# Forming a layer's sample states four heads at a time inside a feed-forward block, instead of beside a run of projections

## The chip, the core and the metric

The kernel runs on one core of one Trainium2 chip. The metric is device microseconds of one execution. The kernel before was timed at 1905.67 us, the median of three runs (1899.02, 1905.67 and 1908.37 us). The engines are named as in the profile: PE is the matrix engine (PEld its weight loads), DVE the vector engine, ACT the scalar engine, POOL the GpSimd engine and SP the engine whose queue issues nearly all transfers. Each engine works through its own instructions strictly in the order in which they were written to it. A semaphore holds an instruction back until what it needs is done, and holds back all that stands behind it on that engine too.

## The reference, cut to what matters

Two layers are computed for 512 prompt tokens and 8 sample tokens with shared weights. Layer 0 mixes with attention and a state-space model, layer 1 with a gated delta rule (16 value heads, 128 by 128 state each). A SwiGLU block (1024 to 2816 and back) follows each layer. For a sample token, the delta rule is one step per head:

```python
def step(s, inp):
    u0_c, kcd_c, attn_c, qg_c, kdec_c, gl_c = inp
    u = u0_c - jnp.einsum('bhik,bhkv->bhiv', kcd_c, s)
    o = jnp.einsum('bhik,bhkv->bhiv', qg_c, s) + jnp.einsum('bhij,bhjv->bhiv', attn_c, u)
    s = s * gl_c[..., None, None] + jnp.einsum('bhjk,bhjv->bhkv', kdec_c, u)
    return s, o
```

With one token per sample, the new state of a head is the old state times a decay, plus the outer product of the key and the vector u. The new states of 8 samples and 16 heads (128 by 128 each, 8.4 MB in all) are an output of the program, `sgs`. Nothing else in the program reads them: the sample's output `o` is worked out earlier from the old states.

## The kernel before

Activations lie transposed: 128 partitions by 520 columns (512 prompt, 8 sample), worked on in two halves of 256 and 264 columns. Every weight matrix is multiplied in three passes of float32r. A weight tile of 4 by 128 rows and 128 columns is split into a high part `whi` (a cast, L317 on ACT or L318 on DVE) and the remainder `wlo` (a subtraction, L193 on POOL or DVE), and each pair of tiles meets the two parts of the activations in three matmuls. One output tile of 128 features with eight k-tiles is 48 matmuls (8 k-tiles, 3 passes, 2 halves), all at L296 (`lin`). Raw weights come by 1 MB loads into two buffers, `raw`. There are four buffers of `whi` and of `wlo`, so the splits run at most four ahead of PE.

Layer 1 ends with its z projections: 16 tiles, each read out of PSUM and gated by `l1_gate` (the intermediate tiles `sq`, with the last product written as `p` or `X`). Beside the first of them `l1_sample` runs the samples' step against the old states, and leaves the vectors u in DRAM (`ud`). In the kernel before, `l1_sample_state` stands in program order between the two groups of eight z tiles. It takes 16 steps, one per sample and half of the heads. A step loads 8 heads of old state into `Hh` (512 KB), loads u spread to all partitions into `cs` (512 KB), multiplies by the decay on POOL (128 by 1024 elements), adds key times u in four DVE instructions (128 by 256 each, L309), and stores 512 KB.

Then come the output projection (768 matmuls with `w_gdn_out`), the norms, and the second feed-forward block, `ffn(1)`. It opens with a group: two gate tiles and two up tiles, run half after half so that PE has work while the norm of the second half is unfinished. The group's second up-weights borrow `b4` and `cs` as split buffers. Ten rounds follow, p from 1 to 10, each of two gate tiles and two up tiles; then comes the down projection. In this block every cast of a weight tile is on DVE, and so are two of three remainders; POOL has the third. DVE also reads the results out of PSUM.

The order of the instructions on each engine is set at build time. A scheduler walks the program with its own estimate of durations and appends to each engine whichever instruction it thinks is ready first. Where it thinks that a result will be there, it may place the instruction that needs it ahead of others.

Of the kernel before, what the change touches and what calls it, by code (L numbers as in the profile page):

```python
# [13 lines left out]
ALU = mybir.AluOpType  # L14
# [6 lines left out]
NS = 8  # L21
# [103 lines left out]
def KN(n, v, *others):  # L125

    return KNOBS.get(n, v)
# [95 lines left out]
class Ker:  # L223
# [103 lines left out]
    def lin(s, w, xh, xl, nkt, halves=(0, 1), ps=None):  # L327

        ps = ps or {h: s.acc()[:, 0:HW[h]] for h in halves}
        for n, (kt, hi, lo) in enumerate(w):  # L330
            for lhs, x, st, sp in ((hi, xh, n == 0, False), (hi, xl, False, False), (lo, xh, False, n == nkt - 1)):
                for h in halves:
                    s.mm(ps[h], lhs, x(kt, h), st, sp)
        return ps
# [752 lines left out]
    def ffn(s, l):  # L1087
        nc = s.nc
        g, u, d = s.i["w_ffn_gate"][l], s.i["w_ffn_up"][l], s.i["w_ffn_down"][l]
# [24 lines left out]
        s.lo_pool = KN("lp_f%d" % l, 1, 2, 3)  # L1114
        s.hi_v = KN("hv_f%d" % l, 0, 2, 3, 4, 1)
        if l:
            s.new_small()
            sgs = s.small(NT)
        for p in range(11):
            sg = {}  # L1120
            for t in (2 * p, 2 * p + 1):
                ps = first[t] if p == 0 else s.lin(s.W.tile(g, 128 * t, kts), *x, 8, ps=spare(t < 2 + KN("ma_f%d" % l, 0, 1, 2)))
                for h in (0, 1):
                    sl = (s.B("cs", NT * (t % 2), NT) if l == 0 else sgs if t % 2 else s.accT)[:, HALF[h]]
                    gt = s.tmp(HW[h])
                    with s.tc.high_priority():
                        s.tt(gt, ps[h], s.R2[:, HALF[h]], ALU.mult)
                    with s.tc.issue_after(s.norm_ins):
                        ins = s.act(sl, gt, AF.Silu)
                    sg[t, h] = sl  # L1130
                if l == 0 and p:
                    s.W.park(ins)
            for t in (2 * p, 2 * p + 1):
                ps = first[2 + t] if 2 + t < len(first) else s.lin(s.W.tile(u, 128 * t, kts), *x, 8)
                for h in (0, 1):
                    gt = s.tmp(HW[h])
                    with s.tc.high_priority():
                        s.tt(gt, sg[t, h], ps[h], ALU.mult)
                    a = hh(t, h)
                    ins = s.act(a, gt)  # L1140
                    s.tt(hl(t, h), gt, a.bitcast(F32), ALU.subtract)
                if l == 0 and p:
                    s.W.park(ins)
        while l == 0 and s.W.wait != [None, None]:
            s.W.park(ins)
        s.gen("Hh")
# [97 lines left out]
    def l1(s):  # L1244
        nc = s.nc
# [94 lines left out]
        for g in range(2):  # L1340
            hi, lo = (("p0", "X"), ("p2", "p7"))[g]
            s.gen(hi, lo)
            for j in range(8):
                s.l1_gate(g, j, lin(4096 + 128 * (8 * g + j)), s.lay(hi), s.lay(lo))
            if g == 0:
                s.l1_sample_state()
        s.l1_sample_gate()
        s.X = s.B("p5", 0, KD, NT)
        s.reload()
# [508 lines left out]
            nc.scalar.copy(hi, m)  # L1858
            s.tt(lo, m, hi.bitcast(F32), ALU.subtract)

    def l1_sample_state(s):
        nc, i, o = s.nc, s.i, s.o
        dap = lambda d: d if isinstance(d, bass.AP) else d[:]
        ud = dap(s.ud)
        gb = s.B("ex", 0, 8, 2, 16)
        s.dma(gb, dap(s.sgd).rearrange("(o b) w h -> o b w h", o=1).to_broadcast([128, 8, 2, 16]))
        for n in range(2 * NS):
            b, e = n // 2, n % 2
            S, ub = s.B("Hh", 1024 * (n % 4), 8, 128), s.B("cs", 1024 * (n % 2), 8, 128)
            s.dma(S, i["state_gdn"][0, b, 8 * e:8 * e + 8].rearrange("h k v -> k h v"))  # L1870
            s.dma(ub, ud[b:b + 1, 8 * e:8 * e + 8].to_broadcast([128, 8, 128]))
            s.tt(S, S, gb[:, b, 0, 8 * e:8 * e + 8].unsqueeze(2).to_broadcast([128, 8, 128]), ALU.mult, s.eng(KN("ss%d" % (n % 4), "G", "V")))
            for j in range(4):
                s.stt(S[:, 2 * j:2 * j + 2], ub[:, 2 * j:2 * j + 2], s.kqs[:, 4 * e + j, b, 0:1], S[:, 2 * j:2 * j + 2], ALU.mult, ALU.add)
            s.dma(o["sgs"][0, b, 8 * e:8 * e + 8].rearrange("h k v -> k h v"), S)

def build(tc, ins, outs, stop=None):
# [45 lines left out]
```

## Time and profile before

| what | value |
|---|---|
| median of three runs | 1905.67 us |
| the profiled execution | 1902.11 us, span 1900.3 us |
| mean granted PE clock | 0.961 of full |
| PE busy | 1747.3 us (92%) |
| DVE, ACT, POOL busy | 1180.4 us (62%), 769.5 us (40%), 891.5 us (47%) |
| bytes moved | 300.38 MB, mean 158 GB/s |
| z projections end, output projection runs | about 1374 us to 1478 us of the span |
| gate and up tiles of the second feed-forward | about 1488 to 1722 us |

A row of the table by stages gives the length of a stretch, then the busy time of each engine with the number of its instructions in brackets, then the granted PE clock, the busy share of the 16 DMA engines and the rate of transfers. A row of the timeline gives the start, the length, the engine, the line, the operation with output and inputs, and in square brackets the idle time just before it and what ended that. A row of the chain of waits gives start, length and what the end of the program hung on then. The busy time of PE is modelled and says little; how many matmuls fall in a stretch says more.

### The profile page before, as it was taken

Reading aid. Unit: us, or ns where it says so; the run is one execution under the profiler, and the core shown is the slowest. Engines: PE = TensorE matmul, PEld = TensorE weight load, DVE = VectorE, ACT = ScalarE, POOL = GpSimd, SP = SyncE. Lnnn points to the kernel's source line nnn. Section 1 sums busy time; section 2 is a strip of 40 time slices with the busy share of each in tenths; the row PEclk is TensorE's granted clock in tenths of the full one; section 3 lists DMA queues with packets and bytes.
Section 4 is the critical chain, followed back from the end, with each engine's and each line's share of the span. In section 5 each row is a group of like instructions: output and inputs, shape, how many; then the busy total and the mean of one; then the engine's idle time right before and its main releaser. Section 6 shows DMA issues by size and latency. Waiting matters only on the chain.

```text
span 1900.3 us, 36580 instructions
## 1 busy us (share of the span) xinstructions
PE 1747.3 (92%) x14263; PEld 1660.3 (87%) x14263; DVE 1180.4 (62%) x2325; ACT 769.5 (40%) x1868; POOL 891.5 (47%) x777
## 2 busy tenths in 40 slices
PE   7889999798999999989977798988899899999996
PEld 6888777598999999979977797977789899999996
DVE  6898878538433321178799958888954955453125
ACT  4442245555333333346766565554334411111222
POOL 2465757234666653342343564545668411112452
PEclk8999999898999999999988999999989899999998
DMA  7335765453565553356752123266998333333544
GB/s 259 124 120 179 227 204 165 135 171 108 167 189 182 180 170 93 92 153 211 245 173 84 46 68 93 56 180 188 279 288 229 134 133 134 134 134 128 158 158 151
DMA packets 325967, 300.38 MB, mean 158 GB/s; under 512 B 13761, under 2 KB 299142, under 8 KB 324626
## 3 DMA queue, kind: packets, MB, share of 16 engines
q1 hardware_dynamic: 325142, 297.37, 50.7%
q8 instruction: 112, 1.84, 0.4%
q10 hardware_dynamic: 652, 0.68, 0.1%
q14 instruction: 61, 0.50, 0.1%
HBM read 261.98 MB, written 72.52 MB: 176 GB/s over the span
## 4 chain that ended last, share of the span: by engine, by line
PE 52%; DVE 19%; DMA 7%; ACT 4%; issue 3%; POOL 1%; SPq 0%; DVEq 0%; ACTq 0%; POOLq 0%
PE acc L296 46%; PE ma L296 3%; DVE p L302 3%; PE mb L296 2%; DVE sq L309 2%; DVE cs L309 2%; DMA raw<-in_w_ffn_down_dram 2%; DVE b L302 1%; ACT L312 1%; DVE wlo L193 1%; DVE Hh L309 1%; DVE Hl L309 1%; DVE p L309 1%; DVE p L1496 1%; PE mb L299 1%
## 5 line engine op out<-in xcount | busy, mean ns | idle before, releaser
L193 POOL TENSOR_TENSOR wlo<-raw,whi 128x512 fp32r<-128x512 f32 (+2 forms) x342 | 456.2, 1337 | 594.1 <-ACT whi L317 296.7
L296 PE MATMUL acc<-Hl,whi 128*128 128x256 f32 (+1 forms) x2576 | 564.5, 292 | 36.1 <-DVE cs L302 18.0
L296 PEld LDWEIGHTS acc<-Hl,whi 128*128 128x128 f32 x2576 | 420.7, 193 | 53.1 <-issue 20.5
L317 ACT CAST whi<-raw 128x512 fp32r<-128x512 f32 (+3 forms) x392 | 234.8, 603 | 436.4 <-PE acc L296 343.6
L296 PE MATMUL acc<-Hh,whi 128*128 128x256 f32 (+1 forms) x1824 | 387.0, 287 | 3.8 <-DVE cs L302 2.0
L296 PE MATMUL acc<-Hh,wlo 128*128 128x256 f32 (+1 forms) x1824 | 389.4, 288 | 0.0
L296 PEld LDWEIGHTS acc<-Hh,whi 128*128 128x128 f32 x1824 | 292.7, 191 | 8.3 <-issue 4.8
L296 PEld LDWEIGHTS acc<-Hh,wlo 128*128 128x128 f32 x1824 | 293.2, 191 | 7.6 <-issue 6.7
L296 PE MATMUL acc<-bm,whi 128*128 128x256 f32 (+1 forms) x1136 | 236.1, 291 | 0.1
L296 PE MATMUL acc<-p,whi 128*128 128x264 f32 (+1 forms) x1280 | 230.0, 287 | 3.9 <-ACT p L1858 1.6
L318 DVE CAST whi<-raw 128x512 fp32r<-128x512 f32 x131 | 61.7, 472 | 253.2 <-PE acc L296 195.9
L193 DVE TENSOR_TENSOR wlo<-raw,whi 128x512 fp32r<-128x512 f32 (+1 forms) x141 | 112.9, 802 | 140.6 <-ACT whi L317 135.5
L296 PEld LDWEIGHTS acc<-p,whi 128*128 128x128 f32 x1280 | 190.3, 192 | 5.6 <-ACT p L1858 1.9
L296 PEld LDWEIGHTS acc<-bm,whi 128*128 128x128 f32 x1136 | 182.9, 195 | 2.4 <-issue 1.6
L296 PE MATMUL acc<-Hl,wlo 128*128 128x256 f32 (+1 forms) x752 | 171.1, 297 | 1.0 <-DMA wlo<-pk 0.5
L296 PE MATMUL acc<-p,wlo 128*128 128x256 f32 (+1 forms) x704 | 164.0, 287 | 8.0 <-DVE wlo L193 7.1
L296 PEld LDWEIGHTS acc<-Hl,wlo 128*128 128x128 f32 x752 | 127.6, 198 | 3.3 <-issue 1.2
L296 PEld LDWEIGHTS acc<-p,wlo 128*128 128x128 f32 x704 | 119.5, 192 | 9.2 <-DVE wlo L193 7.9
L296 PE MATMUL acc<-X,whi 128*128 128x264 f32 (+1 forms) x512 | 100.1, 290 | 2.6 <-DVE X L302 1.3
L309 DVE SCALAR_TENSOR_TENSOR cs<-cs,cw 128x512 f32<-128x512 f32 x100 | 90.6, 906 | 12.0 <-POOL cs L302 7.0
L296 PEld LDWEIGHTS acc<-X,whi 128*128 128x128 f32 x512 | 80.3, 195 | 4.1 <-ACT X L312 2.4
L309 DVE SCALAR_TENSOR_TENSOR Hh<-cs,CS,Hh 128x256 f32<-128x256 f32 x64 | 53.2, 894 | 26.9 <-POOL Hh L302 26.7
(467 smaller groups left out, 3010.0 us busy)
## 6 DMA issues: line engine op xcount, KB each, us to landing
raw<-in_w_gdn_in_dram SPq DMA_DIRECT2D x24, 1024.0 KB
raw<-in_w_ffn_gate_dram SPq DMA_DIRECT2D x22, 1024.0 KB
raw<-in_w_ffn_up_dram SPq DMA_DIRECT2D x22, 1024.0 KB
raw<-in_w_ffn_down_dram SPq DMA_DIRECT2D x20, 1024.0 KB
raw<-in_w_hyb_in_dram SPq DMA_DIRECT2D x16, 1024.0 KB
out_sv_dram<-in_cache_attn_v_dram SPq DMA_DIRECT2D x16, 1023.0 KB
out_sk_dram<-in_cache_attn_k_dram SPq DMA_DIRECT2D x16, 1023.0 KB
cs<-in_w_gdn_in_dram SPq DMA_DIRECT2D x40, 256.0 KB
```

The source lines that it names most:

```text
L193: eng.tensor_tensor(out=lo[:, :nk, d:d + n], in0=raw[:, :, o:o + n], in1=hi[:, :nk, d:d + n].bitcast(F32), op=ALU.subtract)
L296: s.nc.tensor.matmul(out, lhsT=lhsT, rhs=rhs, start=start, stop=stop, skip_group_check=skip)
L299: s.nc.tensor.transpose(out, in_, s.ident[0:in_.shape[0], 0:in_.shape[0]])
L302: return (eng or s.nc.vector).tensor_tensor(out=out, in0=a, in1=b, op=op).ins
L309: return s.nc.vector.scalar_tensor_tensor(out=out, in0=a, scalar=sc, in1=b, op0=op0, op1=op1).ins
L312: return s.nc.scalar.activation(out=out, in_=in_, func=f, **kw).ins
L317: return s.nc.scalar.copy(out, in_).ins
L318: return (s.nc.vector if e == "V" else s.nc.gpsimd).tensor_copy(out, in_).ins
L1496: nc.vector.transpose(out=xt[pr], in_=A[pr, :, pr].rearrange("p y j -> p j y"))
```

## The change

The new states are no longer formed beside the z projections. `l1_sample_state` becomes a generator, `state_steps`, which the second feed-forward advances by one step after each tile of rounds 1 to 10, until its 34 turns are used up. The pieces are half as large: 32 steps of four heads. A turn stores the states of two steps ago, computes the step before, and loads the next one. A step has one state load, one load of u and one store (256 KB each), one POOL multiplication of 128 by 512, and two DVE instructions of 128 by 256. States lie in four buffers of `cs`, u in two buffers of `b4` that the opening group's weights used, and the decays in the small tile instead of `ex`. The multiplications are on POOL, as before. The bytes and the arithmetic are the same as before; only the number of instructions differs: 32 POOL instructions of half the size in place of 16, the same 64 on DVE, 96 transfers of 256 KB in place of 48 of 512 KB.

```diff
@@ ffn
         if l:
+            s.gen("cs")
             s.new_small()
             sgs = s.small(NT)
+            states = s.state_steps()
...
                 if l == 0 and p:
                     s.W.park(ins)
+                if l and p:
+                    next(states, None)
...
                 if l == 0 and p:
                     s.W.park(ins)
+                if l and p:
+                    next(states, None)
+        for _ in states if l else ():
+            pass
@@ l1
                 s.l1_gate(g, j, lin(4096 + 128 * (8 * g + j)), s.lay(hi), s.lay(lo))
-            if g == 0:
-                s.l1_sample_state()
@@
-    def l1_sample_state(s):
...
-        gb = s.B("ex", 0, 8, 2, 16)
+    def state_steps(s):
...
+        gb = s.small(8, 2, 16)
...
-        for n in range(2 * NS):
-            b, e = n // 2, n % 2
-            S, ub = s.B("Hh", 1024 * (n % 4), 8, 128), s.B("cs", 1024 * (n % 2), 8, 128)
-            s.dma(S, i["state_gdn"][0, b, 8 * e:8 * e + 8].rearrange("h k v -> k h v"))
-            s.dma(ub, ud[b:b + 1, 8 * e:8 * e + 8].to_broadcast([128, 8, 128]))
-            s.tt(S, S, gb[:, b, 0, 8 * e:8 * e + 8].unsqueeze(2).to_broadcast([128, 8, 128]), ALU.mult, s.eng(KN("ss%d" % (n % 4), "G", "V")))
-            for j in range(4):
-                s.stt(S[:, 2 * j:2 * j + 2], ub[:, 2 * j:2 * j + 2], s.kqs[:, 4 * e + j, b, 0:1], S[:, 2 * j:2 * j + 2], ALU.mult, ALU.add)
-            s.dma(o["sgs"][0, b, 8 * e:8 * e + 8].rearrange("h k v -> k h v"), S)
+        S = lambda n: s.B("cs", 512 * (n % 4), 4, 128)
+        ub = lambda n: s.B("b4", 2080 + 512 * (n % 2), 4, 128)
+        at = lambda n: (n // 4, slice(4 * (n % 4), 4 * (n % 4) + 4))
+        state = lambda t, n: t[0, at(n)[0], at(n)[1]].rearrange("h k v -> k h v")
+        for n in range(4 * NS + 2):
+            with s.tc.issue_after(s.last_load):
+                if n > 1:
+                    s.dma(state(o["sgs"], n - 2), S(n - 2))
+                if 0 < n < 4 * NS + 1:
+                    t, (b, h) = S(n - 1), at(n - 1)
+                    s.tt(t, t, gb[:, b, 0, h].unsqueeze(2).to_broadcast([128, 4, 128]), ALU.mult, s.nc.gpsimd)
+                    for j in range(2):
+                        v = slice(2 * j, 2 * j + 2)
+                        s.stt(t[:, v], ub(n - 1)[:, v], s.kqs[:, h.start // 2 + j, b, 0:1], t[:, v], ALU.mult, ALU.add)
+                if n < 4 * NS:
+                    b, h = at(n)
+                    s.dma(S(n), state(i["state_gdn"], n))
+                    s.dma(ub(n), ud[b:b + 1, h].to_broadcast([128, 4, 128]))
+            yield
```

What the scheduler makes of it shows first on SP, beside the z projections. `raw` are weight loads, `ud` the vectors u, `out_sgs` the stores. Before, from the store of u on:

```order
L324 DMA ud<-acc 8x8x128 x2
L324 DMA Hh<-in_state_gdn_dram 128x8x128
L324 DMA cs<-ud 128x1024 x2
L324 DMA out_sgs_dram<-Hh 128x8x128
L324 DMA cs<-ud 128x1024
L324 DMA out_sgs_dram<-Hh 128x8x128
L324 DMA cs<-ud 128x1024
L324 DMA Hh<-in_state_gdn_dram 128x8x128
L324 DMA raw<-in_w_gdn_in_dram 128x8x256
```

The changed kernel there:

```order
L324 DMA ud<-acc 8x8x128 x2
L324 DMA raw<-in_w_gdn_in_dram 128x8x256
L324 DMA raw<-in_w_gdn_out_dram 128x16x128 x3
L324 DMA p_75<-xd 128x4160
L324 DMA raw<-in_w_gdn_out_dram 128x16x128 x7
L324 DMA raw<-in_w_ffn_gate_dram 128x8x256
```

Weight loads now follow each other, and none stands behind a store of states. The transfers come back on SP in the feed-forward, from the end of the opening group on (`b_16798` is `b4`, which holds u):

```order
L324 DMA raw<-in_w_ffn_up_dram 128x8x256
L324 DMA b_16798<-ud 128x512 x2
L324 DMA cs<-in_state_gdn_dram 128x4x128 x3
L324 DMA raw<-in_w_ffn_gate_dram 128x8x256
L324 DMA cs<-in_state_gdn_dram 128x4x128
L324 DMA out_sv_dram<-in_cache_attn_v_dram 16x16368
L324 DMA out_sgs_dram<-cs 128x4x128
L324 DMA b_16798<-ud 128x512
L324 DMA out_sgs_dram<-cs 128x4x128
L324 DMA b_16798<-ud 128x512
L324 DMA cs<-in_state_gdn_dram 128x4x128 x2
```

Before, the second of these weight loads followed the first with no transfer of states between. The last place is DVE at the same point, where the norm of the second half (`rs`, then its result `R_90`) lets DVE read out the group (`sq<-acc`). Before:

```order
L306 TENSOR_SCALAR rs_16918<-ma 128x264
L302 TENSOR_TENSOR rs_16918<-rs_16918,rs_16919 128x264
L309 SCALAR_TENSOR_TENSOR rs_16918<-rs_16918,rs_16919 128x264
L309 SCALAR_TENSOR_TENSOR R_90<-rs_16918,rs_16919 128x264
L302 TENSOR_TENSOR sq<-acc,R_90 128x264
L302 TENSOR_TENSOR sq<-acc,R_90 128x256
L302 TENSOR_TENSOR sq<-acc,R_90 128x264
L318 CAST whi<-raw 128x512
```

The changed kernel:

```order
L309 SCALAR_TENSOR_TENSOR rs_16789<-rs_16789,rs_16790 128x264
L309 SCALAR_TENSOR_TENSOR cs<-b_16798,CS,cs 128x256
L309 SCALAR_TENSOR_TENSOR R_90<-rs_16789,rs_16790 128x264
L309 SCALAR_TENSOR_TENSOR cs<-b_16798,CS,cs 128x256
L318 CAST whi<-raw 128x512
L302 TENSOR_TENSOR sq<-acc,R_90 128x264
L302 TENSOR_TENSOR sq<-acc,R_90 128x256
L302 TENSOR_TENSOR sq<-acc,R_90 128x264
L309 SCALAR_TENSOR_TENSOR cs<-b_16798,CS,cs 128x256 x2
L193 TENSOR_TENSOR wlo<-raw,whi 128x512
```

The first state's two DVE instructions now stand around `R_90`, ahead of the cast, and the second state's two ahead of the remainder `wlo`. In the rounds that follow, DVE has four such pairs in each.

More of the change, by code (lines that the diff above doesn't have):

```diff
@@ L1859, in l1_sample_gate @@
             s.tt(lo, m, hi.bitcast(F32), ALU.subtract)
-    def l1_sample_state(s):
-        nc, i, o = s.nc, s.i, s.o
+    def state_steps(s):
+        i, o = s.i, s.o
         dap = lambda d: d if isinstance(d, bass.AP) else d[:]
         ud = dap(s.ud)
-        gb = s.B("ex", 0, 8, 2, 16)
+        gb = s.small(8, 2, 16)
         s.dma(gb, dap(s.sgd).rearrange("(o b) w h -> o b w h", o=1).to_broadcast([128, 8, 2, 16]))
-        for n in range(2 * NS):
-            b, e = n // 2, n % 2
-            S, ub = s.B("Hh", 1024 * (n % 4), 8, 128), s.B("cs", 1024 * (n % 2), 8, 128)
-            s.dma(S, i["state_gdn"][0, b, 8 * e:8 * e + 8].rearrange("h k v -> k h v"))
-            s.dma(ub, ud[b:b + 1, 8 * e:8 * e + 8].to_broadcast([128, 8, 128]))
-            s.tt(S, S, gb[:, b, 0, 8 * e:8 * e + 8].unsqueeze(2).to_broadcast([128, 8, 128]), ALU.mult, s.eng(KN("ss%d" % (n % 4), "G", "V")))
-            for j in range(4):
-                s.stt(S[:, 2 * j:2 * j + 2], ub[:, 2 * j:2 * j + 2], s.kqs[:, 4 * e + j, b, 0:1], S[:, 2 * j:2 * j + 2], ALU.mult, ALU.add)
-            s.dma(o["sgs"][0, b, 8 * e:8 * e + 8].rearrange("h k v -> k h v"), S)
+        S = lambda n: s.B("cs", 512 * (n % 4), 4, 128)
[17 more added lines that the diff above has]
+            yield
 def build(tc, ins, outs, stop=None):
```

## The prediction

> **What bounds the kernel now.** I read the page first, then the busy time by stages, and in the stages with idle PE the waits and the timeline.
>
> ```profile
> PE 1747.3 (92%) x14263; PEld 1660.3 (87%) x14263; DVE 1180.4 (62%) x2325; ACT 769.5 (40%) x1868; POOL 891.5 (47%) x777
> ```
>
> PE is the bound over the whole program, so the question is where it runs below its pace, and whether the states are why. The stages around the change (length; busy PE, PEld, DVE, ACT, POOL with counts; granted clock, DMA share, GB/s):
>
> ```profile
> 1302.00:1310.00 8.00, 8.00 (x69) 8.00 (x68) 6.95 (x14) 3.79 (x9) 4.06 (x5) 1.00 0.15 35
> ...
> 1314.00:1322.00 8.00, 3.05 (x23) 2.87 (x23) 6.15 (x13) 4.41 (x9) 5.82 (x4) 0.89 0.88 250
> 1322.00:1326.00 4.00, 4.00 (x20) 4.00 (x20) 3.52 (x4) 1.74 (x5) 3.90 (x3) 0.50 0.00 0
> 1326.00:1386.00 60.00, 47.43 (x332) 44.70 (x331) 57.09 (x92) 18.70 (x44) 37.24 (x27) 0.87 0.92 258
> 1386.00:1392.00 6.00, 6.00 (x27) 6.00 (x28) 3.25 (x9) 1.24 (x2) 1.28 (x1) 0.50 1.05 389
> 1392.00:1464.00 72.00, 72.00 (x603) 71.97 (x602) 28.97 (x24) 25.82 (x54) 59.13 (x47) 1.00 0.87 244
> 1530.00:1626.00 96.00, 96.00 (x801) 96.00 (x800) 47.91 (x110) 13.55 (x36) 14.71 (x12) 1.00 0.39 132
> 1626.00:1722.00 96.00, 96.00 (x801) 96.00 (x800) 47.21 (x106) 12.87 (x34) 14.93 (x12) 1.00 0.39 132
> ```
>
> In the output projection and in the feed-forward PE does 603 matmuls in 72 us and 801 in 96: 0.1194 and 0.1199 us each, at full clock. The z projections ran at that pace too, up to 1310, with 69 in 8 us. From 1314 to 1386 they do not: 375 matmuls in 72 us, beside a DVE that is busy for 95% of the row from 1326 on.
>
> ```profile
> PE acc L296 <- DVE sq L309: 6.4, 5, 1.7
> PE mb L299 <- DVE acc L306: 4.9, 1, 4.9
> ...
> 1308.72 0.28 DVE L306 TENSOR_SCALAR acc<-acc,CS 128x128 f32<-128x128 f32 x1
> 1311.27 1.99 DVE L309 SCALAR_TENSOR_TENSOR acc<-acc,CS 128x128 f32<-128x128 f32 x1
> 1313.17 2.12 DVE L302 TENSOR_TENSOR X<-sq,p 128x256 fp32r<-128x256 f32 x1
> 1319.28 1.91 DVE L306 TENSOR_SCALAR acc<-acc,CS 128x128 f32<-128x128 f32 x1
> 1311.02 3.99 POOL L302 TENSOR_TENSOR Hh<-Hh,ex 128x1024 f32<-128x1024 f32 x2 [0.28 <-DMA ex<-sgd]
> ```
>
> The waits of PE from 1310 to 1390 are on DVE: the z gates (`sq`), and the samples' chain (`acc`), which one transposition on PE needs. The next rows, of DVE and POOL, say why DVE is late: 128 by 128 took 0.28 us before POOL began on the states at 1311.02, and 1.9 to 2.1 us while it was on them. So the states cost the z gates twice, by their own DVE instructions and by making others long:
>
> ```profile
> L309 DVE SCALAR_TENSOR_TENSOR Hh<-cs,CS,Hh 128x256 f32<-128x256 f32 x32 | 21.0, 713 | 0.2 <-DMA cs<-ud 0.2
> L309 DVE SCALAR_TENSOR_TENSOR sq<-acc,R 128x256 f32<-128x256 f32 (+1 forms) x16 | 6.7, 418 | 0.4
> ...
> L302 POOL TENSOR_TENSOR Hh<-Hh,ex 128x1024 f32<-128x1024 f32 x16 | 32.4, 2027 | 3.3 <-DMA Hh<-in_state_gdn_dram 3.0 <-DMA ex<-sgd 0.3
> ...
> 1386.01 3.24 DVE L309 SCALAR_TENSOR_TENSOR Hh<-cs,CS,Hh 128x256 f32<-128x256 f32 x8
> ```
>
> The two rows with DVE count 1314 to 1386 alone: the states have 21.0 of its 72 us, 0.71 us each, while reads of PSUM (`sq<-acc`) stay at 0.42. The other half of the 64 came after 1386, beside the output projection, where PE waited for none of it; eight of them with POOL idle took 0.41 us each (last row).
>
> **What the change takes away.** Against 0.1194 us a matmul the stretches lose: 8 − 23 × 0.1194 = 5.3 us; 4 − 20 × 0.1194 = 1.6 (half clock); 60 − 332 × 0.1194 = 20.4; 6 − 27 × 0.1194 = 2.8 (half clock again). That is 30.1 us from 1314 to 1392. Not all of it is the states': at the end of z, PE must wait for the last tile's gate before it can go on.
>
> ```profile
> 1380.88 0.58 PE L296 MATMUL acc<-p,whi 128*128 128x256 f32 x1 [1.09 <-ACT p L317]
> 1384.09 0.59 PE L296 MATMUL acc<-p,whi 128*128 128x264 f32 x1 [1.60 <-ACT p L1858]
> 1386.00 0.59 PE L296 MATMUL acc<-X,whi 128*128 128x264 f32 x1 [1.32 <-DVE X L302]
> ```
>
> These are 4.0 us of such waits. Without the POOL work they shrink, but the chain from PSUM through tanh to the split stays, and some of the half clock behind it. I leave 4 us of the 30.1 in place and count **−26 us**, with −30 and −12 as ends (the latter in a rival below). The transfers go with it: 24 MB leave a stretch whose DMA share was 0.92, so nothing new is late there, and SP's weight loads stand behind no store any more.
>
> **What the feed-forward pays: the opening.** Here DVE sets the time at one place before the change:
>
> ```profile
> 1510.50 0.61 PE L296 MATMUL ma<-acc,cst 128*128 128x264 f32 x2
> 1515.30 0.45 DVE R L309
> 1515.77 1.10 DVE L302 TENSOR_TENSOR sq<-acc,R 128x264 f32<-128x264 f32 x3
> ...
> 1516.87 0.34 DVE whi L318
> 1517.22 0.04 issue
> 1517.26 0.75 PE acc L296 x4
> ...
> 1517.79 0.68 DVE L193 TENSOR_TENSOR wlo<-raw,whi 128x512 fp32r<-128x512 f32 x1
> ```
>
> The norm's result, three readings of PSUM and one cast end just when PE wants that cast: PE idles 0.4 us before 1517.26. The first remainder follows by 1518.5. In the changed order the first state stands before `R_90` and a second pair before the remainder, and DVE cannot pass them. Their data start late: u's buffers in `b4` and the states' in `cs` come free only when PE has finished the group, at about 1510.6. The nearest price for a 256 KB load of this shape, spread to all partitions, is the first of these rows; a 512 KB one on a full queue is the second:
>
> ```profile
> 1101.83 4.39 DMA b<-gqd
> ...
> 1331.21 7.12 DMA cs<-ud
> ...
> 1330.00:1440.00 110.00, 97.43 (x729) 94.70 (x729) 0.91 0.99 285
> ```
>
> The last row is the same stage with the matmuls' line alone: the DMA engines, full, move 285 GB/s, so 256 KB take 0.92 us. The first state is third on SP: 1510.6 + 4.4 + 2 × 0.92 = 1516.8. POOL needs half of 2.03 us for it (1517.8). Then DVE does the first half of the state (0.41), `R_90` (0.45), the second half (0.41) and the cast (0.34): 1519.5 instead of 1517.2. The remainder comes after three readings (1.1), two more halves (0.8) and its own 0.68: 1522.1 instead of 1518.5. So PE loses 3.6 us at this tile. It then needs PSUM banks that DVE reads late, an estimated 1.4 us more, and an idle PE can run at half clock afterwards: 1.6 us lost from 1322, 2.8 from 1386, here 2. I take **+7 us**. Ends: +1.5 if the loads land before `R_90`'s turn (only three instructions ahead), +14 if the first takes 7.1 us and the four states queued before the next read of PSUM hold DVE a second time.
>
> **The rounds.** One round is 192 matmuls, 23.0 us. DVE works 95.1 us in the 192 us of the last two stage rows, 11.4 a round. Four states add eight halves, 3.3 us.
>
> ```profile
> L193 POOL TENSOR_TENSOR wlo<-raw,whi 128x512 fp32r<-128x512 f32 x23 | 29.6, 1289 | 168.6 <-DVE whi L318 168.6
> L318 DVE CAST whi<-raw 128x512 fp32r<-128x512 f32 x67 | 28.6, 428 | 94.9 <-PE acc L296 86.9 <-issue 6.4 <-PE ma L296 1.7
> ```
>
> These rows are 1530 to 1722. POOL has 29.6 us of work in 192, so four times 1.0 to 1.3 us more a round find room. If each of the four makes DVE wait for its whole length, some 1.2 us, DVE reaches 11.4 + 3.3 + 4.8 = 19.5 of 23.0. DVE's casts wait 86.9 us for PE: the splits are four tiles ahead, and an instruction late by a few microseconds costs PE nothing. Transfers: share 0.39 makes 9.0 us a round; four states of 0.79 MB at 285 GB/s add 11.0, together 20.0 of 23.0. SP sends each weight load behind two stores that wait for DVE, and the loads have one raw buffer (11.5 us) in hand. I take **+2 us** for all ten rounds, with 0 and +10 as ends. The down projection starts after the last state and is left as it was.
>
> **Sum.** 1902.1 (profiled) − 26 + 7 + 2 = 1885 us; the median of the runs lies 3.6 us higher than the profiled execution, so **1889 us**.
>
> **The rivals.**
>
> 1. *The opening costs next to nothing.* The loads are half the size of the one in the second price row and the queue is empty then, which speaks for it; the 4.39 us row speaks against it. With +1.5 there and nothing lost in the rounds, 1902.1 − 26 + 1.5 = 1878, as a median 1881.
> 2. *z has another bound below the states.* DVE was busy 87% from 1302 to 1310 without any state, and POOL splits all z weights. Then only the 5.3, the 1.6 and a third of 20.4 come back, −13: 1902.1 − 13 + 9 = 1898, median 1902. Against it: 69 matmuls in those 8 us.
> 3. *DVE becomes the bound of the rounds.* POOL has 29.6 / 8.35 rounds = 3.5 us a round and gets 4.8 more; were DVE shut out for all of that time, it would need 11.4 + 3.3 + 8.3 = 23.0, and each wait for a late u on top is a loss. At 2.5 us a round, 8 rounds lose 20: 1902.1 − 26 + 7 + 20 = 1903, median 1907. Against it: the reads of PSUM above kept 0.42 us beside a busy POOL, so DVE isn't shut out for all of that time. [...]
> 4. *Slower: transfers set the round.* Place: the queue that weights share with states in rounds 1 to 8. If four states take more than 14 us of transfers, not 11, the round is 23 us or more, and every state load delays a weight load. At 18 us a round lasts 27: 8 × 4 = 32 us, 1902.1 − 26 + 7 + 32 = 1915, median 1919. It decides for slower from 2.4 us a round, that is below 0.79 × 4 / 16.4 = 193 GB/s for the states. Against it: 250 and 285 GB/s in rows above that are mostly state transfers.
>
> [...]
>
> **How the numbers follow.** Forecast 0.52, rival 1 0.20, rival 2 0.09, rival 3 0.11, rival 4 0.08. What a measurement of this kernel can tell from no change is about 0.5%, 9.5 us. Faster by more (below 1896): the forecast and rival 1, 0.72. Within: rivals 2 and half of 3 and some of the forecast's bad end, 0.17. Slower by more (above 1915): rival 4 and the tail of 3, 0.11. The forecast's own range, from the ends of its terms, is 1878 to 1900; the range for 8 in 10 takes in rivals 1 to 3 in part, 1876 to 1905.
>
> **What would show it.** Right: from the samples' transposition to the end of the output projection about 0.12 us a matmul, with no `Hh` work on POOL and the remaining short waits at the end of z; a PE wait of 3 to 7 us on DVE `whi` or `wlo` just after the opening group, and DVE's first `cs<-b` row waiting on POOL or a transfer; then 801 matmuls in 96 us, DMA share near 0.87, DVE near 0.8. Wrong: PE waits spread over rounds 2 to 9, a clock below 1.00 there, or weight loads on the chain of waits; or z still below pace with POOL free of states.

## The result, and the profile after

| | before | changed |
|---|---|---|
| median of 11 runs each, us | 1906.82 (1899.02 to 1910.98) | 1897.14 (1886.62 to 1899.92) |
| ratio, 95% interval | | 0.9948 (0.9934 to 0.9962) |
| the same pair again (11 and 6 runs) | 1900.97 | 1888.80; 0.9928 (0.9906 to 0.9951) |
| profiled executions: time, span | 1902.11, 1900.3 | 1886.62, 1884.8; the second 1889.16, 1887.3 |

The change gains 9.7 us in the first comparison and 12.2 us in the second, where 17 were forecast. The first profile of the changed kernel is the shortest of its runs, so a second one ("changed, again") stands beside it below.

**The z projections and the output projection.** First the waits of PE from 1310 to 1400 of the changed kernel (us in total, times, longest), then the busy time of the stretch from the samples' transposition to the first residual (length; busy PE, PEld, DVE, ACT, POOL with counts; granted clock, DMA share, GB/s):

```profile
PE mb L299 <- DVE acc L306: 2.9, 1, 2.9
...
1317.60:1435.90 118.30, 118.30 (x988) 118.28 (x987) 37.04 (x66) 49.10 (x106) 71.70 (x64) 1.00 0.39 114
```

VectorE, ScalarE, GpSimd, SyncE and TensorE in the text are DVE, ACT, POOL, SP and PE of the rows. One wait of 2.9 us is left of all that stood there, and behind it PE runs for 118 us without a gap, 0.1197 us a matmul, through the end of z and the output projection. The marks of the stretch are the transposition on `mb` and the first matmul of the residual's norm, here of before, of the changed kernel and of the changed kernel again, from the timelines of PE:

```profile
L299 PE MATMUL mb<-cst,acc x1: 445/445/445, 1321.3 to 1321.3; 128*128 128x128 f32 x1
1463.74 0.59 PE L296 MATMUL mb<-acc,cst 128*128 128x256 f32 x2
```

```profile
L299 PE MATMUL mb<-cst,acc x1: 299/299/299, 1317.3 to 1317.3; 128*128 128x128 f32 x1
1435.53 0.59 PE L296 MATMUL mb<-acc,cst 128*128 128x256 f32 x2
```

```profile
L299 PE MATMUL mb<-cst,acc x1: 299/299/299, 1316.8 to 1316.8; 128*128 128x128 f32 x1
1436.63 0.59 PE L296 MATMUL mb<-acc,cst 128*128 128x256 f32 x2
```

That is 142.4 us before and 118.2 and 119.8 after, 24.2 and 22.6 less; the wait ahead of it fell from 4.9 to 2.9 and 2.8. Together the stage gained 26.2 and 24.7 us.

**The feed-forward.** From the second mark on I cut the same three lengths in every profile: 85 us (the norm and the opening), 115 us and 85 us (the rounds). The rows count PE's matmuls of line 296 (length; PE busy with count; clock, DMA share, GB/s). Before:

```profile
1463.74:1548.74 85.00, 79.23 (x603) 0.94 0.43 143
1548.74:1663.74 115.00, 115.00 (x959) 1.00 0.41 138
1663.74:1748.74 85.00, 85.00 (x710) 1.00 0.38 125
```

The changed kernel, and again:

```profile
1435.53:1520.53 85.00, 76.37 (x563) 0.92 0.60 189
1520.53:1635.53 115.00, 111.84 (x913) 1.00 0.84 269
1635.53:1720.53 85.00, 84.50 (x698) 1.00 0.57 189
```

```profile
1436.63:1521.63 85.00, 77.43 (x555) 0.88 0.58 187
1521.63:1636.63 115.00, 111.55 (x910) 1.00 0.83 267
1636.63:1721.63 85.00, 84.26 (x696) 1.00 0.58 193
```

At 0.12 us a matmul the opening lost 40 and 48 matmuls, 4.8 and 5.8 us; the rounds lost 46 + 12 and 49 + 14, 7.0 and 7.6 us. The gain at z was paid back by 11.8 and 13.4 us, where 9 were forecast, and most of what was not forecast is in the rounds.

What VectorE does there, in the 120 us from 1540 to 1660 of before and of the changed kernel, again (busy us, mean ns of one; idle before them and what ended it). A "half" is one of the two VectorE instructions that form a state (L309), a "remainder" the subtraction that gives `wlo` (L193):

```profile
1540.00:1660.00 120.00, 120.00 (x1001) 120.00 (x1000) 58.75 (x132) 15.90 (x42) 16.90 (x14) 1.00 0.43 147
...
L193 DVE TENSOR_TENSOR wlo<-raw,whi 128x512 fp32r<-128x512 f32 x28 | 19.3, 688 | 1.8 <-DVE whi L318 0.5
L318 DVE CAST whi<-raw 128x512 fp32r<-128x512 f32 x42 | 18.0, 428 | 60.1 <-PE acc L296 55.5 <-issue 4.6
```

```profile
1540.00:1660.00 120.00, 115.81 (x942) 113.58 (x941) 81.75 (x165) 15.29 (x40) 39.14 (x34) 1.00 0.82 262
...
L309 DVE SCALAR_TENSOR_TENSOR cs<-b,CS,cs 128x256 f32<-128x256 f32 x40 | 24.3, 645 | 34.6 <-POOL cs L302 24.2 <-DMA b<-ud 10.4
L193 DVE TENSOR_TENSOR wlo<-raw,whi 128x512 fp32r<-128x512 f32 x26 | 21.5, 825 | 1.0
L318 DVE CAST whi<-raw 128x512 fp32r<-128x512 f32 x39 | 18.1, 467 | 3.6 <-PE acc L296 3.6
```

The telling number is the last one: before, VectorE's casts waited 55.5 us for PE, so VectorE was ahead. Now they wait 3.6 us. Its busy time went from 58.75 to 81.75 us, and 34.6 us more it stands before a half of a state until GpSimd's product or u is there. That makes 116.4 of 120 us: VectorE has become as tight as PE, and PE now waits there for VectorE's reads of PSUM (`sq`): 4.2 us in seven waits, where it waited for nothing before.

### The profile page after: what moved, and what is told of

Read it like the earlier page. It is cut to its first block, busy times and chain, and to the rows that moved or that the text cites. A ratio compares the mean times of both kernels' runs of the same rounds, so it can differ in the third digit from the quotient of the medians.

```text
span 1884.8 us, 36666 instructions
## 1 busy us (share of the span) xinstructions
PE 1744.3 (93%) x14263; PEld 1656.7 (88%) x14263; DVE 1160.9 (62%) x2325; ACT 769.3 (41%) x1868; POOL 890.8 (47%) x793
## 4 chain that ended last, share of the span: by engine, by line
PE 50%; DVE 18%; DMA 9%; ACT 4%; issue 4%; POOL 2%; SPq 1%; DVEq 0%; ACTq 0%; POOLq 0%
PE acc L296 43%; PE ma L296 4%; DVE p L302 3%; DVE cs L309 3%; PE mb L296 2%; DMA b<-ud 2%; DMA raw<-in_w_ffn_down_dram 1%; DVE wlo L193 1%; ACT L312 1%; DMA cs<-in_state_gdn_dram 1%; POOL cs L302 1%; SPq L324 1%; DVE b L302 1%; DVE Hl L309 1%; PE mb L299 1%
## 5 line engine op out<-in xcount | busy, mean ns | idle before, releaser
L193 POOL TENSOR_TENSOR wlo<-raw,whi 128x512 fp32r<-128x512 f32 (+2 forms) x342 | 453.2, 1328 | 504.9 <-ACT whi L317 304.3
L193 DVE TENSOR_TENSOR wlo<-raw,whi 128x512 fp32r<-128x512 f32 (+1 forms) x141 | 117.6, 835 | 140.3 <-ACT whi L317 137.7
L309 DVE SCALAR_TENSOR_TENSOR cs<-cs,cw 128x512 f32<-128x512 f32 x100 | 90.4, 905 | 12.0 <-POOL cs L302 7.0
L302 POOL TENSOR_TENSOR cs<-cs,small 128x512 f32<-128x512 f32 x48 | 55.1, 1152 | 87.8 <-DMA cs<-in_state_gdn_dram 68.8
```

The source lines that it names most:

```text
L193: eng.tensor_tensor(out=lo[:, :nk, d:d + n], in0=raw[:, :, o:o + n], in1=hi[:, :nk, d:d + n].bitcast(F32), op=ALU.subtract)
L302: return (eng or s.nc.vector).tensor_tensor(out=out, in0=a, in1=b, op=op).ins
L309: return s.nc.vector.scalar_tensor_tensor(out=out, in0=a, scalar=sc, in1=b, op0=op0, op1=op1).ins
```

## The experiments

All ratios are to the kernel before, timed beside the run on the same chip, with 95% intervals. The runs e1 to e4, e5 to e8 and e9 to e12 are three groups on three chips; between groups the ratios compare, and the medians less well. "Opening" and "rounds" are the matmuls that the one profiled execution lacks in the three lengths above, against 603, 959 and 710, times 0.12 us. One execution varies by some us (the two of the changed kernel: 4.8 and 5.8, 7.0 and 7.6), so they show where, and the ratio how much. In e5, e8 and e10 the further buffer is the one in which a small term of the last norm lies (`ex`), so that term has other values there. The run e2 leaves the new states out, and e7 forms all but the first two steps' with the u of another step.

The expectations and the text below call their theories by letters. O: the opening loses the time. T: the transfers come late. L: GpSimd's work lengthens VectorE's beside it, as at z before the change, where one form on `acc` (128 by 128) took 0.28 us until GpSimd began on the states and 1.91 us beside them. K: VectorE waits for GpSimd's product, which stands in GpSimd's queue behind other work. Q: an instruction that waits in GpSimd's queue holds the weight remainder behind it, and through it the next weight load and the loads of u and states behind that.

| run | ratio | median us | opening us | rounds us |
|---|---|---|---|---|
| e1 changed, again | 0.9928 (0.9906 to 0.9951) | 1888.80 | 5.8 | 7.6 |
| e2 no states | 0.9868 (0.9845 to 0.9890) | 1878.01 | 0 | 0 |
| e3 from round 2 | 0.9901 (0.9874 to 0.9928) | 1883.74 | 0 | 11.8 |
| e4 decay on ScalarE | 0.9878 (0.9855 to 0.9900) | 1878.62 | 2.5 | 0 |
| e5 e4 + idle GpSimd work on u | 0.9941 (0.9923 to 0.9960) | 1889.04 | 7.1 | 10.3 |
| e6 e4, one column on GpSimd | 0.9923 (0.9903 to 0.9943) | 1887.62 | 4.1 | 4.9 |
| e7 u loaded twice only | 0.9928 (0.9907 to 0.9950) | 1888.26 | 5.5 | 3.8 |
| e8 loads two steps ahead | 0.9923 (0.9899 to 0.9947) | 1884.91 | 5.8 | 2.2 |
| e9 e4 + idle 128x4 on u | 0.9895 (0.9872 to 0.9918) | 1883.59 | 4.1 | 2.5 |
| e10 e4 + idle GpSimd work, no transfer | 0.9908 (0.9885 to 0.9931) | 1886.13 | 4.7 | 5.0 |
| e11 state loads issued by ScalarE | 0.9979 (0.9960 to 0.9998) | 1899.16 | 4.9 | 18.5 |
| e12 e4 + e3 | 0.9862 (0.9840 to 0.9884) | 1876.06 | 0 | 1.7 |

**e1, the change again.** No edit.

> The changed kernel once more, unchanged. The profiled execution of the first result (span 1884.8 us) is 10 us shorter than the median of its runs (1897.1), so a second profile can show where an ordinary execution loses the rest. Theory T (late transfers, in-order VectorE): z again near 118 us for 985 matmuls after the samples' transposition, and the additional time in rounds 1 to 8 of the second feed-forward, as PE waits on the reads of PSUM (DVE sq) with DVE's u and state rows waiting on DMA just ahead. Theory O (the opening): the additional time lies at 1495 to 1540, as a longer wait on whi or wlo. Median 1897, within 4 us, under both.

Measured 1888.8 us, 0.9928; its interval overlaps that of the first comparison. The median came 8 us under the 1897 that was expected; the kernel before was 5.9 us faster in this group too (1900.97, after 1906.82). The larger part of the loss is in the rounds (7.6 us, after 5.8 in the opening), as theory T has it, with PE waits on `sq` and VectorE's waits on states ahead of them; but whether the transfers were the cause was open.

**e2, without the states.**

```diff
-            states = s.state_steps()
+            states = iter(())
```

> The changed kernel with the samples' new gated-delta states left out altogether (their loads, POOL and VectorE work and stores; that output isn't written). What is left is the program without the work that was moved: it gives what the states cost in the feed-forward. By the steps of the prediction, with z at its 28 us gain: 1906.8 - 28 = about 1879 us, so the states would cost 18 us in the feed-forward in an ordinary execution of the change (1897). If the states are not what holds the change back (the loss comes from something else in the second feed-forward, or z gave less in ordinary executions), it stays above 1890. Rounds 2 to 9 should show 801 matmuls in 96 us.

Measured 1878.0, as expected from z alone, and the feed-forward ran as in the kernel before:

```profile
1438.57:1523.57 85.00, 78.28 (x605) 0.96 0.42 143
1523.57:1638.57 115.00, 115.00 (x960) 1.00 0.40 138
1638.57:1723.57 85.00, 85.00 (x709) 1.00 0.38 127
```

So the states are the whole of the cost in the feed-forward, 10.8 us between the medians of e1 and e2 (18 was expected, worked out from the slower median of the first comparison), and nothing else in the change is seen to cost time there. Against the kernel before, e2 is 23.0 us faster: that is what the states had cost beside z.

**e3, states from round 2.**

```diff
-                if l and p:
+                if l and p > 1:
```

(at both places)

> The changed kernel with the first two rounds' steps left off: the states begin with round 2 instead of round 1 (2 p > 2), everything else as in the change, and the last states go behind round 10 as far as they have no step left. Theory O (the opening costs 5 to 7 us because the first states stand before R_90 and the remainder): 4 to 6 us below the change, about 1892, and the PE wait of some 1.2 to 2.7 us behind the opening group gone. Theory T (the rounds lose because transfers come late, at whatever round they begin): at most 2 us below the change, about 1895 to 1899, the same waits on reads of PSUM appearing one round later.

The opening's loss went to zero, and the ratio improved by 0.0027 (5.1 us between the medians, within the 4 to 6 of theory O), but the intervals overlap; the profiled execution, the longest of its runs, lost 11.8 us in its rounds in place of 7.6. Theory O holds for the opening; it is not the larger part. What makes the opening late is not what the prediction said. VectorE (with the first decay of POOL) behind the norm's last group, which began at 1482.03; the first fence is the changed kernel, the second the kernel before, where it began at 1510.50:

```profile
1485.97 3.42 POOL L302 TENSOR_TENSOR cs<-cs,small 128x512 f32<-128x512 f32 x3
...
1486.00 1.29 DVE L302 TENSOR_TENSOR rs<-rs,rs 128x264 f32<-128x264 f32 x1 [1.08 <-ACT rs L312]
1487.33 1.16 DVE L309 SCALAR_TENSOR_TENSOR rs<-rs,rs 128x264 f32<-128x264 f32 x1
1488.41 1.26 DVE L309 SCALAR_TENSOR_TENSOR cs<-b,CS,cs 128x256 f32<-128x256 f32 x1
1489.59 0.42 DVE L309 SCALAR_TENSOR_TENSOR R<-rs,rs 128x264 f32<-128x264 f32 x1
```

```profile
1514.37 0.43 DVE L302 TENSOR_TENSOR rs<-rs,rs 128x264 f32<-128x264 f32 x1 [1.08 <-ACT rs L312]
1514.84 0.43 DVE L309 SCALAR_TENSOR_TENSOR rs<-rs,rs 128x264 f32<-128x264 f32 x1
1515.30 0.43 DVE L309 SCALAR_TENSOR_TENSOR R<-rs,rs 128x264 f32<-128x264 f32 x1
```

The first three states were there in time: POOL starts on them 3.9 us after the group, and VectorE waits for none. But beside POOL's three decays the norm's two instructions take 1.29 and 1.16 us in place of 0.43, and the half 1.26; `R` starts 7.6 us after the group, not 4.8: 1.6 us of the difference is the norm's own instructions, and 1.3 the half in front of `R`. PE then waited 2.74 us for a read of PSUM and 1.22 for a remainder.

**e4, the decay on ScalarE.**

```diff
-                    s.tt(t, t, gb[:, b, 0, h].unsqueeze(2).to_broadcast([128, 4, 128]), ALU.mult, s.nc.gpsimd)
+                    for j in range(4):
+                        s.act(t[:, j], t[:, j], scale=gb[:, b, 0, h.start + j:h.start + j + 1])
```

> The changed kernel with the states' decay on ScalarE (four multiplications of 128x128 by a scalar per partition) in place of GpSimd's one of 128x512. ScalarE has time to spare in the feed-forward (13 us of 96). Theory L (VectorE and GpSimd shut each other out, so that GpSimd's 1.2 us a state lengthens remainders and state sums): the time falls by 5 us or more, to about 1890, and the state's halves on DVE fall from 0.62 to about 0.42 us. Theory T (DVE waits for u and states that arrive late, whoever multiplies): within 3 us of the change, 1895 to 1900, DVE's halves shorter and its waits on DMA as long as before.

1878.6 us: the time of the program without states, and the intervals of e4 and of the change don't meet; the gain is larger than theory L expected (about 1890). The rounds lose nothing, with the same transfers:

```profile
1540.00:1660.00 120.00, 120.00 (x1001) 120.00 (x1000) 76.06 (x172) 40.94 (x122) 17.97 (x14) 1.00 0.82 267
...
L193 DVE TENSOR_TENSOR wlo<-raw,whi 128x512 fp32r<-128x512 f32 x28 | 20.1, 718 | 0.7
L309 DVE SCALAR_TENSOR_TENSOR cs<-b,CS,cs 128x256 f32<-128x256 f32 x40 | 18.9, 505 | 30.8 <-ACT cs L312 20.4 <-DMA b<-ud 7.2 <-ACT small L312 3.1
L318 DVE CAST whi<-raw 128x512 fp32r<-128x512 f32 x42 | 18.1, 434 | 12.7 <-PE acc L296 12.6
```

1001 matmuls, as before, at a DMA share of 0.82, the same as the changed kernel's. Theory T falls: the bytes are not the bound. VectorE still waits 30.8 us for states. But its halves take 0.505 us and not 0.645, its remainders 0.718 and not 0.825, and the casts are ahead of PE by 12.6 us again. That speaks for theory L; but taking the decay off GpSimd also takes an instruction that waits for a transfer out of GpSimd's queue. The next two runs were meant to part these.

**e5 and e6, the work and the queue.** e5 is e4 with

```diff
+        s.gen("ex")
+        dm = s.B("ex", 0, 4, 128)
...
+                    s.tt(dm, ub(n - 1), gb[:, b, 0, h].unsqueeze(2).to_broadcast([128, 4, 128]), ALU.mult, s.nc.gpsimd)
```

and e6 is e4 with column 0 of each head on GpSimd:

```diff
+                    s.tt(t[:, :, 0:1], t[:, :, 0:1], gb[:, b, 0, h].unsqueeze(2), ALU.mult, s.nc.gpsimd)
                     for j in range(4):
-                        s.act(t[:, j], t[:, j], scale=gb[:, b, 0, h.start + j:h.start + j + 1])
+                        s.act(t[:, j, 1:128], t[:, j, 1:128], scale=gb[:, b, 0, h.start + j:h.start + j + 1])
```

> The decay is on ScalarE, as in the run before, and GpSimd does an instruction of the size and form of the decay (128x512, two SBUF inputs, from u's buffer to an unused one) whose result nobody uses. The order on TensorE, VectorE and SyncE is that of the decay on ScalarE. Theory L (GpSimd's work itself makes VectorE's instructions with two SBUF inputs long): most of the 10 us between the decay on ScalarE (0.988 of before) and the change (0.993) come back, 0.992 or more, and the states' halves go from 0.51 to above 0.6 us. Theory K (the link: VectorE waits for GpSimd's result, which stands in a queue behind other work): it stays at 0.988 to 0.989.

> The opposite of the run with idle GpSimd work: ScalarE does columns 1 to 127 of each head and GpSimd column 0 alone (128x4 instead of 128x512), so that the link from the state's load through GpSimd to VectorE stays and its long instruction goes. Theory K (the link): near the change, 0.992 or more of before. Theory L (the long GpSimd instruction): near the decay on ScalarE, 0.988 to 0.989.

Both are as slow as the change: 0.9941 and 0.9923, and both intervals lie apart from e4's. The scheduler gave e4 another order on VectorE than the change has; e5 and e6 keep e4's order on PE, VectorE and SyncE, so the order is not what e4 gained by. e5 shows theory L at its strongest; its halves:

```profile
L309 DVE SCALAR_TENSOR_TENSOR cs<-b,CS,cs 128x256 f32<-128x256 f32 x38 | 36.3, 994 | 24.5 <-ACT cs L312 12.3 <-DMA b<-ud 8.9 <-ACT small L312 3.1
...
L302 POOL TENSOR_TENSOR ex<-b,small 128x512 f32<-128x512 f32 x19 | 21.1, 1108 | 56.7 <-DMA b<-ud 54.2 <-DVE wlo L193 1.4 <-DVE whi L318 1.1
```

0.994 us in place of 0.505: 38 × 0.489 = 18.6 us more, beside 21.1 us of GpSimd's work, which waits for the same u (54.2 us of its waits). VectorE's remainders, with two inputs in SBUF like the halves, did not grow (0.710 us after 0.718 in e4), nor its casts (0.436 after 0.434); GpSimd's own remainders took 1.344 us after 1.290. So the added work lengthens the halves here; by what mechanism is not shown. But e6, with next to no work of the states on GpSimd (5.5 us of 120), was not expected by L, so L alone does not do. Theory K expected this time, but its wait is not in e6's rows: from 1540 to 1660 VectorE's halves were last held by ScalarE (26.5 us) and u (14.1), by GpSimd for 1.6 us, and that by a weight remainder. VectorE's work on the halves hardly grew over e4 (20.2 us after 18.9); its waits ahead of them did, from 30.8 to 42.3 us. Where they may come from is seen in one round. VectorE's cast, GpSimd and the weight loads of SyncE, of e6 and then of e4:

```profile
1597.39 0.43 DVE L318 CAST whi<-raw 128x512 fp32r<-128x512 f32 x1 [0.98 <-PE acc L296]
...
1602.57 0.20 POOL L302 TENSOR_TENSOR cs<-cs,small 128x4 f32<-128x4 f32 x1 [7.85 <-DMA cs<-in_state_gdn_dram]
1602.72 1.29 POOL L193 TENSOR_TENSOR wlo<-raw,whi 128x512 fp32r<-128x512 f32 x1
...
1592.29 0.37 SPq L324 DMA_DIRECT2D raw<-in_w_ffn_gate_dram  x1
1604.03 0.37 SPq L324 DMA_DIRECT2D raw<-in_w_ffn_up_dram  x1
```

```profile
1589.00 0.43 DVE L318 CAST whi<-raw 128x512 fp32r<-128x512 f32 x1 [1.65 <-PE acc L296]
...
1589.60 1.29 POOL L193 TENSOR_TENSOR wlo<-raw,whi 128x512 fp32r<-128x512 f32 x1 [4.64 <-DVE whi L318]
...
1582.49 0.37 SPq L324 DMA_DIRECT2D raw<-in_w_ffn_gate_dram  x1
1590.97 0.37 SPq L324 DMA_DIRECT2D raw<-in_w_ffn_up_dram  x1
```

In both, the weight load leaves SyncE just as GpSimd's remainder ends and frees the raw buffer. In e6 that remainder stands behind the one-column product, which waits 7.85 us for its state: the remainder starts 4.9 us after its cast has ended, in e4 0.2 us after. The load leaves 11.7 us after the one before, in e4 8.5 us, and the first load of a state behind it leaves SyncE 13.9 us after the gate load, in e4 12.0. This is not so in every round: of e6's loads of `w_ffn_up` from 1540 to 1640 one leaves 11.7 us after the gate load ahead of it and the others 8.8 to 9.3, in e4 8.3 to 9.0. I called this theory Q; e9 and e11 test it. The runs e7 and e8 were on record before it, with e5 and e6.

**e7 and e8, the transfers.** e7:

```diff
-                    s.dma(ub(n), ud[b:b + 1, h].to_broadcast([128, 4, 128]))
+                    if n < 2:
+                        s.dma(ub(n), ud[b:b + 1, h].to_broadcast([128, 4, 128]))
```

e8, where the loop also runs one step longer and the halves take `ub(n - 2)`:

```diff
-        ub = lambda n: s.B("b4", 2080 + 512 * (n % 2), 4, 128)
+        s.gen("ex")
+        ub = lambda n: s.B("b4", 2080 + 512 * (n % 3), 4, 128) if n % 3 < 2 else s.B("ex", 0, 4, 128)
...
-                if n > 1:
-                    s.dma(state(o["sgs"], n - 2), S(n - 2))
-                if 0 < n < 4 * NS + 1:
-                    t, (b, h) = S(n - 1), at(n - 1)
+                if n > 2:
+                    s.dma(state(o["sgs"], n - 3), S(n - 3))
+                if 1 < n < 4 * NS + 2:
+                    t, (b, h) = S(n - 2), at(n - 2)
```

> The changed kernel with u loaded for the first two steps only; all later states are formed with these two, so the samples' new states are other numbers. A third of the new transfers (256 KB of 768 a step) and VectorE's wait for u are gone. Theory T (late transfers): VectorE loses its waits on u (10 us in 1540 to 1660, and what queues in front of the state loads), the time falls 5 us or more, to 0.990 of before or less. Theory L: within 3 us of the change, 0.992 to 0.994, since the waits move from u to the state or to GpSimd.

> The changed kernel with the loads two steps ahead of the sum in place of one: u has a third buffer, each store comes a step later. The decay stays on GpSimd. Theory T: VectorE no longer waits for u or a state, and the time falls 5 us or more, to 0.990 of before or less. Theory L: VectorE's halves and remainders stay long, the time falls by 3 us at most.

0.9928 and 0.9923: neither can be told from the change, and theory T's 0.990 was not reached. So neither u's bytes and its 10 us of waits nor this edit for a step of lead are shown to decide. A smaller gain is not ruled out: in the one profiled execution of each the rounds lost 3.8 and 2.2 us, after 7.0 and 7.6 (in e8 it is the second shortest of six). Nor did e8 bring the states earlier: GpSimd waited 57.7 us for them, in e1 56.4. SyncE met another wait, for the stores that leave the states' buffers; its queue's waits from 1540 to 1660:

```profile
SPq L324 <- DMA out_sgs_dram<-cs: 30.0, 13, 4.4
```

Four state buffers are not enough here for two steps of lead; more were not tried, for want of room.

**e9 and e10, the queue and the work apart.** Both are e4 with one more GpSimd instruction per step. e9, into four columns that nobody reads:

```diff
+        dm = s.small(4, 1)
+                    s.tt(dm, ub(n - 1)[:, :, 0:1], gb[:, b, 0, h].unsqueeze(2), ALU.mult, s.nc.gpsimd)
```

e10:

```diff
+        s.gen("ex")
+        dm = s.B("ex", 0, 4, 128)
...
+                    s.tt(dm, S(n - 2) if n > 1 else t, gb[:, b, 0, h].unsqueeze(2).to_broadcast([128, 4, 128]), ALU.mult, s.nc.gpsimd)
```

> Theory Q, new after the last runs: what costs is GpSimd's queue. An instruction that waits there for a transfer holds the weight remainder behind it, the raw weight buffer comes free late, the next weight load on SyncE is issued late, and the loads of u and states behind it are late in turn. Here ScalarE does the whole decay; GpSimd does one instruction of 128x4 a step on u's buffer, into columns that nobody reads: no link to VectorE, no work to speak of, only a wait for u in GpSimd's queue. TensorE, VectorE and SyncE have the order of the decay on ScalarE. Theory Q: 0.991 to 0.993 of before, as with one column of the decay on GpSimd. Theory K (VectorE's wait for GpSimd's result) and theory L (GpSimd's work): both 0.988, as with the decay on ScalarE.

> ScalarE does the whole decay; GpSimd does an instruction of the decay's size and form on the state of a step earlier, which lies in its buffer already, into a buffer that nobody needs: the work without a wait for a transfer. Theory Q: 0.988 to 0.989 of before, GpSimd's remainders ahead of time though VectorE's halves get longer (0.6 us or more). Theory L: 0.991 or more.

0.9895 and 0.9908. Q alone misses e9 (it came too cheap) and e10 (too dear), L alone misses e6, K alone e5. By the times, L with K fits these runs as well as L with Q; against K speaks only the list of waits of e6. And e10 is not the work without a wait: its instruction waits for no transfer, but from 1540 to 1660 it stood 54.4 us in GpSimd's queue until VectorE's halves of an earlier step were done. Each of the two lies above e4 by 0.0017 and 0.0030, with intervals that overlap e4's, so neither is shown alone. Both at once (e5) is 0.0063 above, and there the intervals are apart. In the profiled rounds it is 2.5 us for the wait, 5.0 for the work, 10.3 for both. e9 has e4's order on PE, VectorE and SyncE too; e10's differs a little on VectorE and by one load on SyncE.

**e11, the states' loads on another queue.**

```diff
-                    s.dma(S(n), state(i["state_gdn"], n))
+                    s.dma(S(n), state(i["state_gdn"], n), s.nc.scalar)
```

> The changed kernel, decay on GpSimd, with the states' loads issued by ScalarE instead of SyncE; u and the stores stay on SyncE, the scheduler orders the rest anew. If the loads are late because they stand on SyncE behind a weight load that waits for its raw buffer (the circle of theory Q), GpSimd's wait for states (56 us in 1540 to 1660) falls by half or more and the time to 0.990 of before or less. If they are late for the transfer itself, or the cost is GpSimd's work (theory L): 0.992 to 0.994, as the change.

0.9979, worse than e1, and neither of the two times that were expected. GpSimd waited 45.7 us for states in place of 56.4, not half, and a new queue held the work; waits from 1540 to 1660:

```profile
DVE cs L309 <- DMA b<-ud: 31.8, 9, 5.4
...
ACT small L312 <- DMA cs<-in_state_gdn_dram: 17.0, 2, 8.9
```

The loads now stand on ScalarE ahead of the activations that the products of the feed-forward need, and u is later than ever (31.8 us, after 10.4). So the circle of theory Q was not broken by this, and whether SyncE's order feeds it stays open.

**e12, both edits that gained.** The edit of e4 and the edit of e3 together.

> The two edits that gained, together: decay on ScalarE and the first state with round 2 instead of round 1. With the decay on ScalarE the rounds ran at full pace, and 2.8 us of waits of TensorE on whi and wlo were left at the opening (1480 to 1545). If these go: 1.5 to 2.5 us below the decay on ScalarE, 0.9865 to 0.987 of before, the time of the program without the states. If the opening isn't what is left: 0.988.

1876.1 us, 0.9862, the shortest of all and within its interval the time without states. It beats the changed kernel (0.9928 and 0.9948) and the one before. Between it and e4 the intervals overlap.

## Why the prediction was right, and where it was off

**The signs.** Of what the prediction named as showing it right, z's signs came: 0.12 us a matmul and no work of the states on POOL. For the rounds its sign of being wrong came: waits of PE spread over them, 942 matmuls in 120 us of e1 where 1001 were done before, and VectorE occupied for 0.97 of the time with its waits for states, where near 0.8 was forecast.

**z, "−26".** Right in size: −26.2 and −24.7. The 4 us that I left in place are there, but elsewhere: the last gates' waits went to nothing, and 2.9 of the 4.9 us before the samples' transposition stayed. Rival 2 (another bound below the states) is out: 988 matmuls in 118.3 us.

**Opening, "+7".** 4.8 and 5.8 us: near, but by luck, since the reason was wrong. The step that failed is "the first state is third on SP: 1516.8", 6.3 us after the group: it came after less than 3.9. What made `R` and the cast late is POOL's work beside the norm's own instructions (0.43 to 1.29 us) and beside the half in front of `R` (1.26 us, forecast 0.41), the lengthening that I had read at z and not carried over to here. The 1.4 us for late reads of PSUM rested on no row; PE waited 2.74 us for such a read. So "a PE wait of 3 to 7 us on `whi` or `wlo`" was seen as 2.74 on `sq` and 1.22 on `wlo`. e3 and e12 show that a start in round 2 removes it. Rival 1 is out.

**Rounds, "+2".** This is the term that was mis-sized: 7.0 and 7.6 us. Two sentences failed. "DVE reaches 19.5 of 23.0": it is 116.4 of 120, which is 22.3 of 23.0, since the halves cost 0.645 us and not 0.41, and the waits for a state 34.6 us for 20 states, 1.7 each and not 1.2. And "an instruction late by a few microseconds costs PE nothing": that rested on the casts' 86.9 us of waiting for PE, but that waiting is the slack itself, and 3.6 of 55.5 us were left of it. Rival 3 named the right engine and a price nearly three times too high (20 us, where 7.0 and 7.6 were lost), and the lengthening beside GpSimd that it reckoned with is in the rows: halves 0.645 us in e1 and 0.505 in e4, remainders 0.825 and 0.718. I gave it 0.11 because reads of PSUM keep their 0.42 us, which they did (0.415 to 0.423 from 1540 to 1660 in every run), but remainders and halves were what counted. What it did not have is a cost with hardly any work on GpSimd (e6).

**Rival 4, transfers set the round.** Out: e4 ran the rounds at full pace at a DMA share of 0.82.

**The sum.** −26 + 7 + 2 = −17; measured from profile to profile −15.5 and −13.0, from median to median −9.7 and −12.2. The first profile of the changed kernel lies 10.5 us under its median, so the medians' larger loss of the first comparison has no trace of its own. That e1's median, 1888.80, meets the forecast 1889 is in part luck: the kernel before ran at 1900.97 there and not at 1905.67. Two sums don't come out as written. The ends of the three terms add up to 1877 to 1918 and not to 1878 to 1900 (both medians lie within either), and the terms of rival 2 to 13.7 us and not 13.

**What is shown.** That the states had cost z its time is shown by e2, and that the decay on GpSimd is what the rounds paid for by e4 against e1, with e5 and e6. How the cost divides between GpSimd's work and what waits in its queue stays open: e6 costs 0.0045 over e4 with hardly any work, and e9 and e10 can't be told from e4. Theory Q's chain was followed in one round only.

## What to carry to other kernels

When work is moved to a stage where the bounding engine never waits, read the slack of its feeder: how long the feeder waits for the bounding engine, and subtract the new work at its contended price and each wait for data. From 1540 to 1660 this is 24.3 + 34.6 = 58.9 us in e1, against a slack of 55.5 before, and 18.9 + 30.8 = 49.7 us in e4, which lost nothing. The measure is rough and was worked out afterwards: e7, with 25.8 + 23.8 = 49.6 us, still lost a little. It can pay to put the new step's elementwise part on an engine whose queue doesn't also prepare weights: here four short ScalarE instructions of 0.39 us (e4, 0.9878 of before) were worth more than one GpSimd instruction of 1.1 us (e1, 0.9928). An instruction that is tiny but waits for a transfer can hold up what stands behind it: in e6 one of 0.20 us held a remainder for 4.9.

## What was not expected of the hardware

After a wait of PE of 1.95 us in e7 the granted clock was 0.64 for four microseconds; after one of 1.50 us in e6 it stayed at 1.00. The length of the wait alone doesn't settle it: with one of 1.53 us in e5 the clock was 0.81 in the four microseconds that hold the wait and 0.76 in the next four. PE's rows and the clock of e7, then of e6:

```profile
1618.77 0.73 PE L296 MATMUL acc<-Hh,whi 128*128 128x256 f32 x2 [1.95 <-DVE sq L302]
...
1616.00:1620.00 4.00, 2.05 (x13) 1.69 (x13) 4.00 (x9) 0.77 (x2) 0.97 (x1) 0.93 0.00 0
1620.00:1624.00 4.00, 4.00 (x25) 4.00 (x24) 2.80 (x7) 0.79 (x2) 1.29 (x1) 0.64 0.90 303
```

```profile
1616.39 0.73 PE L296 MATMUL acc<-Hh,whi 128*128 128x256 f32 x2 [1.50 <-DVE sq L302]
...
1600.00:1620.00 20.00, 18.50 (x153) 18.14 (x152) 12.10 (x28) 7.41 (x23) 3.74 (x7) 1.00 0.71 225
1620.00:1640.00 20.00, 19.95 (x167) 19.74 (x165) 11.38 (x27) 7.12 (x22) 3.66 (x7) 1.00 0.92 297
```

In e7 25 matmuls in place of 34 (4.00 us at 0.1194) cost 1 us on top of the wait, half as much again.
